# Decay matrices of a two-way SSD scan: built by VectorE from broadcast rows, or as TensorE products onto a mask in PSUM

## The chip, the cores and the metric

The kernel runs on one core of one Trainium2 chip. The metric is the device time of one execution in microseconds (us). Before the change it is 1887.61 us, the median of three runs (1885.88 to 1889.07). Five engines work side by side, each in its own fixed order: TensorE (PE; its weight loads are PEld), VectorE (DVE), ScalarE (ACT), GpSimd (POOL), and SyncE (SP), which in this kernel issues every DMA.

## The reference

One layer of a hybrid block over 1024 latent tokens of width 1024, with a context of 256 tokens: a modulated RMSNorm, one wide input projection, three branches (a bidirectional Mamba-2 SSD, a Fourier mix, a gated MLP over token chunks), an output projection, and a gated feed-forward with a short convolution. The change is within the SSD, which works on 8 chunks of 128 tokens, 16 heads of width 64 and 2 groups. Cut to what matters:

```
cum  = cumsum(dt * a)                                  # per head, in a chunk
lmat = exp(where(tri_q, cum[q] - cum[s], -inf))        # decay from token s to token q, 128 x 128 per head
cb   = C_q . B_s                                       # one 128 x 128 matrix per chunk and group
y_diag = sum_s cb[q,s] * lmat[q,s] * dt[s] * x[s]      # forward; the same on flipped tokens for backward
y_off  = exp(cum[q]) * C_q . state ;  y = y_diag + y_off
```

For each chunk, group and head both directions are wanted: the forward matrix lives on one side of the diagonal, the backward matrix on the other, and the two are added (on the diagonal both count).

## The kernel before

Matrices are split into a high and a low float32r part, and each projection is three products per 128 rows of depth (helper `mm3`, L147). A projection tile of 128 output channels is 48 products of 128x512 into one of two large PSUM tiles (`ps_big`, two banks each, pool `psm` with 2 buffers). Small PSUM tiles (`ps_small`, one bank) have the tags c, c2, y and t, one buffer each.

After the context and the first group's tiles, `ssd_group(0)` is written, then `group_in(1)` (the projection, convolution and transposes of the second group: tiles B, C and four x tiles, with the four Fourier tiles `f_tile` between them), then `ssd_group(1)`, then the z, u and v tiles. A scheduler merges this into one fixed order per engine. So the projection tiles ("fill tiles" here: `psx`, `psf`, `psz`, `psu`, `psv` by their PSUM names) stand on TensorE between the small products of the SSD groups. A fill x tile goes: 48 products into `psx`; `conv5` (L288: one ScalarE pass, then four VectorE passes that read `psx`); a tanh and a product (`silu_half`); eight transposes `pstx` (`tok_major`, L441) and their copies out.

One chunk step of `ssd_group` (L547 to L583): `pcb` is cb; `po` and `pS` are the products for y_off and for the state, in both directions; `py` is the product of the decay matrices with x. Per half group of four heads (`hg`) the decay matrix comes from two DMA broadcasts of rows of cum (`rload`), per head a ScalarE pass that adds the column's own cum (L561), a VectorE pass with the minimum of both directions (L562), a ScalarE and a VectorE pass for the factor with cb and dt (L564, L565), then one Exp for four heads (L567) and a product on GpSimd (L568). `ro` (L498) are decay rows for y_off, also broadcast by DMA.

Of the kernel before, what the change touches and what calls it, by code (L numbers as in the profile page):

```python
# [32 lines left out]
def hybrid_block_kernel(ctx: ExitStack, tc: tile.TileContext, a, dbg=None):  # L33
# [26 lines left out]
    def bc(ap, shape):  # L60
        return ap.broadcast_to(shape)
# [430 lines left out]
    def rload(c, d_, g, hg, nm, tag):  # L492
        r = s3.tile([P, 4, P], F32, tag=tag, name=f"{nm}{g}{c}{hg}")
        o = d_ * 16 + g * 8 + hg * 4
        SY.dma_start(r, Rd[c, o:o + 4, :].partition_broadcast(P))
        return r
# [37 lines left out]
    def xload(g, c, nm):  # L534
        X = s3.tile([P, 512], F32, tag="X" + nm, name=f"X{nm}{g}{c}", bufs=2 if nm == "f" else 1)
        SY.dma_start(X, Xd[g][c])
        return X

    def ssd_group(g, BT, Bt, CT):
        st0 = []  # L540
        for d_ in range(2):
# [4 lines left out]
        scr[1, g] = s3.tile([P, L], F32, tag="scr", name=f"scr1{g}", bufs=1)
        for c in range(NCH):  # L547
            X = xload(g, c, "f")
            pcb = ps_small(f"pcb{g}{c}", "c")
            PE.matmul(pcb[:, 0:P], BT[:, c * P:(c + 1) * P], CT[:, c * P:(c + 1) * P], start=True, stop=True)  # L550
            cbm = s3.tile([P, 2, P], F32, tag="cbm", name=f"cbm{g}{c}", bufs=1)
            V.tensor_tensor(cbm, bc(pcb[:, 0:P].unsqueeze(1), [P, 2, P]), msk, op=ALU.mult)  # L552
            y_off(g, c, 0, stf, CT, G)
            py = ps_small(f"py{g}{c}", "y")
            for hg in range(2):
                E = rload(c, 0, g, hg, "rf", "rf")
                rs = rload(c, 1, g, hg, "rs", "rs")
                Gm = s3.tile([P, 4, P], F32, tag="G", name=f"G{g}{c}{hg}")
                for h in range(4):
                    f = g * 8 + hg * 4 + h  # L560
                    S.activation(E[:, h, :], E[:, h, :], AF.Identity, bias=ncum[:, c, f:f + 1])  # L561
                    V.scalar_tensor_tensor(E[:, h, :], rs[:, h, :], ncum[:, c, 16 + f:17 + f], E[:, h, :],  # L562
                                           op0=ALU.add, op1=ALU.min)
                    S.activation(Gm[:, h, :], cbm[:, 0, :], AF.Copy, scale=dtl[:, c, f:f + 1])  # L564
                    V.scalar_tensor_tensor(Gm[:, h, :], cbm[:, 1, :], dtl[:, c, 16 + f:17 + f], Gm[:, h, :],  # L565
                                           op0=ALU.mult, op1=ALU.add)
# [30 lines left out]
    xbc_post(10, psb10, CT)  # L597
    n2w, nfw, ssdd, ssdn, fcw, fcb = late_consts()
    Rd = dram.tile([NCH, 32, P], F32, name="Rd")
    psr = ps_small("psr")  # L600
    for i in range(2):
        PE.transpose(out=psr[:, i * P:(i + 1) * P], in_=cums[:, 4 * i:4 * i + 4, :].rearrange("p c h -> p (c h)"),
                     identity=ident)
    Rs_ = ddp.tile([P, 2, P], F32, tag="ul", name="Rs_")
    S.activation(Rs_, psr[:, 0:2 * P].rearrange("p (i q) -> p i q", i=2), AF.Copy)
    SY.dma_start(Rd.rearrange("(i c) h q -> (c h) i q", i=2), Rs_)
    yacc[0] = mpool.tile([P, 4, L], F32, tag="m", name="yacc0")
    for i, ts in enumerate(((9,), (4, 5), (6,), (7,))):
        x_tile(0, i, True)
# [1135 lines left out]
```

## Time and profile before

| | |
|---|---|
| median of three runs | 1887.61 us |
| the profiled execution | 1883.76 us, its span 1882.0 us, mean granted TensorE clock 0.967 |
| busy in the span | PE 1747.4 us (93%), DVE 1383.9 (74%), ACT 859.9 (46%), POOL 856.0 (45%) |
| the SSD groups with their fill tiles | 235.7 to 558 us of the span |

A view by lines gives, per group of equal instructions, the busy time, the mean ns of one, and the idle time of the engine before them with what ended it. A view by windows gives, for a stretch of time, the busy time of each engine and its count of instructions.

### The profile page before, as it was taken

What the parts mean: (1) busy time and instruction counts of PE and PEld (TensorE: products, weight loads), DVE (VectorE), ACT (ScalarE), POOL (GpSimd) and SP (SyncE); (2) the same over time, 40 slices, a digit from 0 to 9 for tenths busy, and PEclk for the clock granted to TensorE, in tenths of its full rate; (3) what the DMA queues carried; (4) which work ended last, traced back from release to release, by engine and by line L of the source; (5) the groups of instructions that cost most, each with busy time, mean ns of one, the idle gap of its engine ahead of it and who ended that gap; (6) DMA issues with size and microseconds to landing.
All of it is one profiled execution on the core that took longest, in us unless ns stands there. A gap on an engine that the chain in (4) does not pass through costs nothing. (4 is left out here: it accounts for less than half of the span.)

```text
span 1882.0 us, 23647 instructions
## 1 busy us (share of the span) xinstructions
PE 1747.4 (93%) x8148; PEld 1409.2 (75%) x8148; DVE 1383.9 (74%) x1983; ACT 859.9 (46%) x1480; POOL 856.0 (45%) x579
## 2 busy tenths in 40 slices
PE   4899998988989989999899999799999999899988
PEld 2688776766668868888688888578888888677777
DVE  7875577777573675557949536998888889967896
ACT  6644355564442344444524234445555455533433
POOL 3322355556531464554645745633333333544553
PEclk9999999999999989999998999899999999999998
DMA  9211365553454225765346464122232225553532
GB/s 336 101 59 61 118 191 159 154 159 116 148 183 160 107 85 184 235 224 184 118 146 201 129 230 140 40 90 96 95 126 104 96 96 174 199 187 106 174 111 90
DMA packets 148064, 268.75 MB, mean 143 GB/s; under 512 B 15836, under 2 KB 56668, under 8 KB 146536
## 3 DMA queue, kind: packets, MB, share of 16 engines
q1 hardware_dynamic: 147944, 267.25, 43.0%
q8 instruction: 64, 1.05, 0.2%
q14 instruction: 56, 0.46, 0.1%
HBM read 209.90 MB, written 57.29 MB: 142 GB/s over the span
## 5 line engine op out<-in xcount | busy, mean ns | idle before, releaser
L293 DVE SCALAR_TENSOR_TENSOR acc<-psx,convw,acc 128x1023 f32<-128x1023 f32 (+1 forms) x48 | 61.3, 1277 | 22.5 <-ACT acc L289 22.1
L562 DVE SCALAR_TENSOR_TENSOR rf<-rs,ncuml,rf 128x128 f32<-128x128 f32 x128 | 52.2, 454 | 32.4 <-ACT rf L561 29.2
L1272 POOL TENSOR_TENSOR pwo<-rwo,pwo 128x512 fp32r<-128x512 f32 x32 | 46.8, 1467 | 48.5 <-ACT pwo L1271 43.4
L857 POOL TENSOR_TENSOR w1up<-A11up,w1up 128x512 fp32r<-128x512 f32 x20 | 26.8, 1342 | 89.8 <-ACT w1up L856 80.6
L568 POOL TENSOR_TENSOR rf<-rf,G 128x512 f32<-128x512 f32 x32 | 46.1, 1442 | 43.1 <-DVE G L565 33.0
L857 POOL TENSOR_TENSOR w7up<-S3up,w7up 128x512 fp32r<-128x512 f32 x20 | 28.8, 1438 | 77.5 <-ACT w7up L856 45.0
L565 DVE SCALAR_TENSOR_TENSOR G<-cbm,dtl,G 128x128 f32<-128x128 f32 x128 | 57.0, 504 | 5.1 <-ACT G L564 5.1
L1561 DVE SCALAR_TENSOR_TENSOR xf<-Yd,g,xf 128x512 f32<-128x512 f32 x64 | 47.1, 743 | 13.0 <-PE Yd L867 12.7
L561 ACT ACTIVATE rf<-rf,ncuml 128x128 f32<-128x128 f32 x128 | 41.1, 389 | 29.5 <-DMA rf<-Rd 29.3
L166 ACT ACTIVATE gh<-gr 128x1024 fp32r<-128x1024 f32 (+1 forms) x36 | 37.1, 1034 | 38.0 <-DMA gr<-Gd 37.1
L157 PE MATMUL pso<-mh,pwo 128*128 128x512 f32 x128 | 50.2, 392 | 0.0
L153 PE MATMUL pso<-mh,pwo 128*128 128x512 f32 x128 | 49.8, 390 | 0.0
L155 PE MATMUL pso<-ml,pwo 128*128 128x512 f32 x128 | 49.8, 389 | 0.0
L517 DVE TENSOR_TENSOR scr<-po,ro 128x512 f32<-128x512 f32 x32 | 21.8, 683 | 35.2 <-ACT ro L504 35.0
L527 PE MATMUL pS<-scr,Bt 128*128 128x512 f32 x56 | 32.9, 671 | 15.4 <-DVE scr L517 12.0
L504 ACT ACTIVATE ro<-ro 128x512 f32<-128x512 f32 x32 | 20.1, 627 | 57.4 <-DMA ro<-Rd 57.1
L564 ACT ACTIVATE G<-cbm,dtl 128x128 f32<-128x128 f32 x128 | 39.6, 388 | 7.4 <-DVE cbm L552 7.4
L167 DVE TENSOR_TENSOR gl<-gr,gh 128x1024 fp32r<-128x1024 f32 (+1 forms) x26 | 39.7, 1527 | 4.2 <-ACT gh L166 3.6
L1477 DVE TENSOR_TENSOR gt<-gt,aa 128x512 f32<-128x512 f32 x44 | 42.5, 967 | 0.1
L1474 ACT ACTIVATE ft<-aa 128x512 f32<-128x512 f32 x44 | 27.8, 631 | 30.0 <-DVE aa L1456 29.0
L529 POOL TENSOR_TENSOR st<-st,etl 128x512 f32<-128x512 f32 x24 | 26.5, 1106 | 31.6 <-DVE st L531 31.6
L857 POOL TENSOR_TENSOR w4up<-A22up,w4up 128x512 fp32r<-128x512 f32 x20 | 30.9, 1544 | 21.4 <-ACT w4up L856 21.4
(1291 smaller groups left out, 6622.6 us busy)
## 6 DMA issues: line engine op xcount, KB each, us to landing
gr<-Gd SPq DMA_DIRECT2D x70, 256.0 KB, 3.7
Gd<-gt SPq DMA_DIRECT2D x10, 1536.0 KB, 5.7
wm<-in_wmod_dram SPq DMA_DIRECT2D x16, 512.0 KB, 9.6
ro<-Rd SPq DMA_DIRECT2D x64, 128.0 KB, 3.3
rf<-Rd SPq DMA_DIRECT2D x32, 256.0 KB, 4.3
rs<-Rd SPq DMA_DIRECT2D x32, 256.0 KB, 3.8
ctanh<-in_wmod_dram SPq DMA_DIRECT2D x32, 256.0 KB, 4.3
crow<-in_wmod_dram SPq DMA_DIRECT2D x32, 256.0 KB, 4.4
```

Of the source, the lines that this page charges most:

```text
L153: PE.matmul(o, wh[:, k, :], xh[:, sl], start=st, stop=False)
L155: PE.matmul(o, wh[:, k, :], xl[:, sl], start=False, stop=False)
L157: last_op["mm"] = PE.matmul(o, wl[:, k, :], xh[:, sl], start=False, stop=sp)
L293: V.scalar_tensor_tensor(acc[:, lo:hi], ps[:, lo + o:hi + o], cw[:, t, j:j + 1], acc[:, lo:hi], op0=ALU.mult, op1=ALU.add)
L561: S.activation(E[:, h, :], E[:, h, :], AF.Identity, bias=ncum[:, c, f:f + 1])
L562: V.scalar_tensor_tensor(E[:, h, :], rs[:, h, :], ncum[:, c, 16 + f:17 + f], E[:, h, :], op0=ALU.add, op1=ALU.min)
L565: V.scalar_tensor_tensor(Gm[:, h, :], cbm[:, 1, :], dtl[:, c, 16 + f:17 + f], Gm[:, h, :], op0=ALU.mult, op1=ALU.add)
L568: G.tensor_tensor(E, E, Gm, op=ALU.mult)
L857: (V if p in on_v else G).tensor_tensor(t[:, 1, :], ap, f32(t)[:, 0, :], op=ALU.subtract)
L1272: G.tensor_tensor(t[:, 1, :], raw, f32(t)[:, 0, :], op=ALU.subtract)
L1477: V.tensor_tensor(gt[:, 2 * q + h, :], gt[:, 2 * q + h, :], aa[:, HS[h]], op=ALU.mult)
L1561: V.scalar_tensor_tensor(xv, src, g2[:, dd:dd + 1], xv, op0=ALU.mult, op1=ALU.add)
```

## The change

The factor dt goes into the exponent: its logarithm (`lds`) less cum is a row per token s, cum a row per token q, and both are written to DRAM as a high and a low part (`Rr`). The exponents of four heads are then one product on TensorE: weights `Lt` of 128 rows, of which 18 are not zero (16 of lds - cum for 8 heads in two parts, 2 of ones), against `Rt` of 128 x 1024 (rows of indicators, and two rows of cum). ScalarE first writes the mask (0 or -1e30) into a PSUM bank (tag t, which nothing else uses in the SSD groups now), and the product is added onto it. ScalarE takes the Exp, VectorE adds the two directions and multiplies with cb. Tag t is no longer free for the transposes of the second group's tiles: they take a large PSUM tile in rotation with the projections.

```diff
     def tok_major(src, nm, dst, tags=("t", "t")):
+        pb = ps_big(f"pst{nm}") if tags is None else None
         for i in range(2):
-            p_ = ps_small(f"pst{nm}{i}", tags[i])
+            p_ = ps_small(f"pst{nm}{i}", tags[i]) if tags else pb[:, 512 * i:512 * i + 512]
...
+        if not tags:
+            S.activation(dst, pb.rearrange("p (c x) -> p c x", c=8), AF.Copy)
...
-        tok_major(ac, f"x{t}", xt_, ("t", "c2" if ctx_too else "t"))
+        tok_major(ac, f"x{t}", xt_, ("t", "c2") if ctx_too else None)
...
-        tok_major(BT, f"b{g}", Bt)
+        tok_major(BT, f"b{g}", Bt, None)
...
+    def exponents(E, c, d_, hg):
+        S.activation(E.rearrange("p (h q) -> p h q", h=4), bc(neg[:, d_].unsqueeze(1), [P, 4, P]), AF.Copy)
+        PE.matmul(E, Lt[c // 2 % 2][:, 2 * (c % 2) + d_, :], Rt[:, 512 * hg:512 * hg + 512], start=False, stop=True,
+                  skip_group_check=True)
+
+    def load_rows(c, g):
+        for d_ in range(2):
+            i = 2 * (c % 2) + d_
+            SY.dma_start(f32(Lt[c // 2 % 2])[32 * i:32 * i + 16, i, :],
+                         Rr[1][c, 2 * d_ + g].rearrange("l h q -> (l h) q"))
+            SY.dma_start(f32(Rt)[32 * i + 16:32 * i + 18], Rr[0][c, 2 * d_ + g].rearrange("l h q -> l (h q)"))
...
             X = xload(g, c, "f")
+            load_rows(c, g)
...
-            cbm = s3.tile([P, 2, P], F32, tag="cbm", name=f"cbm{g}{c}", bufs=1)
-            V.tensor_tensor(cbm, bc(pcb[:, 0:P].unsqueeze(1), [P, 2, P]), msk, op=ALU.mult)
+            cb = s3.tile([P, P], F32, tag="cb", name=f"cb{g}{c}")
+            S.activation(cb, pcb[:, 0:P], AF.Copy)
...
             for hg in range(2):
-                E = rload(c, 0, g, hg, "rf", "rf")
-                rs = rload(c, 1, g, hg, "rs", "rs")
-                Gm = s3.tile([P, 4, P], F32, tag="G", name=f"G{g}{c}{hg}")
-                for h in range(4):
...
-                S.activation(E, E, AF.Exp)
-                G.tensor_tensor(E, E, Gm, op=ALU.mult)
+                ef = s3.tile([P, 512], F32, tag="ef", name=f"ef{g}{c}{hg}", bufs=1)
+                E = ps_small(f"F{g}{c}{hg}", "t")
+                exponents(E, c, 0, hg)
+                S.activation(ef, E, AF.Exp)
+                eb = ps_small(f"E{g}{c}{hg}", "t")
+                exponents(eb, c, 1, hg)
+                S.activation(eb, eb, AF.Exp)
+                V.tensor_tensor(eb, ef, eb, op=ALU.add)
+                w_ = s3.tile([P, 4, P], F32, tag="G", name=f"G{g}{c}{hg}")
+                V.tensor_tensor(w_, eb.rearrange("p (h q) -> p h q", h=4), bc(cb.unsqueeze(1), [P, 4, P]), op=ALU.mult)
...
+    lds = ddp.tile([P, NCH, 32], F32, name="lds", tag="w" + "l")
+    V.tensor_scalar(lds, dtl, 1e-37, None, op0=ALU.max)
+    S.activation(lds, lds, AF.Ln)
+    V.tensor_tensor(lds, lds, cums, op=ALU.subtract)
...
+    for j in range(2):
+        rh = ddp.tile([P, 2, P], F32R, tag=("rl", "t2l")[j], name=f"rh{j}")
...
+                SY.dma_start(Rr[j][4 * i:4 * i + 4, :, q], f32(t)[:, i, :])
```

The new orders follow at three places. First, TensorE at the end of the x tile of `wx5` in the first SSD group. Before:

```order
L155 MATMUL psx_2845<-hl_549,wx5h 128x512 x2
L157 MATMUL psx_2845<-hh_548,wx5l 128x512 x2
L573 MATMUL py_1980<-rf_1981,Xf_1963 64x128 x4
L527 MATMUL pS_2037<-scr_1667,Bt_591 128x512
L153 MATMUL psf_2924<-hh_289,wf3h 128x512 x2
L155 MATMUL psf_2924<-hl_290,wf3h 128x512 x2
```

Now (F and E are the exponent products of the two directions):

```order
L155 MATMUL psx_2735<-hl_549,wx5h 128x512 x2
L157 MATMUL psx_2735<-hh_548,wx5l 128x512 x2
L498 MATMUL E_1974<-Rt,Lt_1694 128x512
L537 MATMUL pS_2083<-scr_1705,Bt_591 128x512
L561 MATMUL pcb_2113<-CT_592,BT_590 128x128
L581 MATMUL py_1968<-G_1979,Xf_1947 64x128 x4
L498 MATMUL F_1986<-Rt,Lt_1694 128x512
L498 MATMUL E_1990<-Rt,Lt_1694 128x512
L446 MATMUL pstx_2795<-cst,acc_2784 128x128 x8
L153 MATMUL psf_2812<-hh_289,wf3h 128x512 x2
```

The transposes of the same tile now stand ahead of the first product of the next fill tile; before, the whole next tile (48 products) stood between the last product of `psx` and its transposes.

Second, TensorE near the end of the second SSD group. Before, the last two `py` stand among products of the v tile `wv1`:

```order
L155 MATMUL psv_4727<-hl_438,wv1h 128x512
L573 MATMUL py_3843<-rf_3844,Xf_3826 64x128 x4
L155 MATMUL psv_4727<-hl_438,wv1h 128x512
L157 MATMUL psv_4727<-hh_437,wv1l 128x512 x2
L153 MATMUL psv_4727<-hh_474,wv1h 128x512 x2
L155 MATMUL psv_4727<-hl_475,wv1h 128x512 x2
L573 MATMUL py_3843<-rf_3871,Xf_3826 64x128 x4
L183 MATMUL rby_4462<-dgy_4456,cst 128x512
L157 MATMUL psv_4727<-hh_474,wv1l 128x512 x2
```

Now the last product of that v tile is followed by this (the first `py` here is the second half of chunk 3 of 8):

```order
L157 MATMUL psv_4467<-hh_548,wv1l 128x512 x2
L581 MATMUL py_3285<-G_3312,Xf_3264 64x128 x4
L498 MATMUL F_3367<-Rt,Lt_1693 128x512
L524 MATMUL po_3438<-CT_2338,st_3402 128x128 x4
L498 MATMUL E_3371<-Rt,Lt_1693 128x512
L537 MATMUL pS_3499<-scr_3023,Bt_2337 128x512
L537 MATMUL pS_3480<-scr_3022,Bt_2337 128x512
L524 MATMUL po_3569<-CT_2338,st_3501 128x128 x4
L581 MATMUL py_3365<-G_3376,Xf_3344 64x128 x4
L498 MATMUL F_3383<-Rt,Lt_1693 128x512
```

Chunks 4 to 7 of the second group, eight pairs of F and E with nine `py`, five `po` and four `pS`, now stand behind the last fill product; the next fill product (`psv` of `wv2`) comes after the Fourier products that follow them.

Third, SyncE at the same place, chunks 6 and 7, now (`Rt` is the load of two rows for each direction, `tabc`, `fT` and `tab` are for the Fourier products that come next):

```order
L506 DMA Rt<-Rr_866 2x1024 x2
L546 DMA Xf_3504<-Xd_581 128x512
L513 DMA ro_3639<-Rd 64x4x128 x2
L768 DMA wsT_4362<-in_wsT_dram 128x128
L770 DMA bsb_4364<-in_bs_dram 128x128
L768 DMA wsT_4457<-in_wsT_dram 128x128
L770 DMA bsb_4459<-in_bs_dram 128x128
L506 DMA Rt<-Rr_866 2x1024 x2
L546 DMA Xf_3584<-Xd_581 128x512
L506 DMA Rt<-Rr_866 2x1024 x2
L1200 DMA Hb_5024<-Hr_252 128x512
```

Each chunk's pair of `Rt` loads stands once, behind a wait for the last exponent product of the chunk before, since all products read all rows of `Rt`.

## Rows read from the trace of the kernel before

**Rows 1.** Windows: length, then busy us (count) per engine, granted clock, DMA.

```profile
235.70:404.00 168.30, 150.28 (x789) 115.08 (x787) 122.19 (x230) 95.97 (x216) 83.85 (x62) 0.99 0.58 165
404.00:558.00 154.00, 137.84 (x667) 101.83 (x668) 107.31 (x186) 75.00 (x166) 91.26 (x66) 0.93 0.47 142
...
720.00:760.00 40.00, 40.00 (x178) 33.11 (x178) 21.65 (x45) 16.71 (x30) 20.20 (x15) 1.00 0.66 211
```

**Rows 2.** Waits of PE, 200 to 560 us: us in total, times, longest.

```profile
PE pS L527 <- DVE scr L517: 12.0, 8, 3.4
```

**Rows 3.** Lines, 235 to 556 us, VectorE, ScalarE and GpSimd in the SSD.

```profile
L565 DVE SCALAR_TENSOR_TENSOR G<-cbm,dtl,G 128x128 f32<-128x128 f32 x128 | 57.0, 504 | 5.1 <-ACT G L564 5.1
L562 DVE SCALAR_TENSOR_TENSOR rf<-rs,ncuml,rf 128x128 f32<-128x128 f32 x128 | 52.2, 454 | 32.4 <-ACT rf L561 29.2 <-DMA rs<-Rd 2.9
L568 POOL TENSOR_TENSOR rf<-rf,G 128x512 f32<-128x512 f32 x32 | 46.1, 1442 | 43.1 <-DVE G L565 33.0 <-PE psx L157 6.2 <-DVE rf L562 3.1
L561 ACT ACTIVATE rf<-rf,ncuml 128x128 f32<-128x128 f32 x128 | 41.1, 389 | 29.5 <-DMA rf<-Rd 29.3
...
L517 DVE TENSOR_TENSOR scr<-po,ro 128x512 f32<-128x512 f32 x32 | 21.8, 683 | 35.2 <-ACT ro L504 35.0 <-issue 0.2
...
L567 ACT ACTIVATE rf<-rf 128x512 f32<-128x512 f32 x32 | 19.9, 623 | 19.7 <-DVE rf L562 19.5
```

**Rows 4.** The same view, TensorE's products in the SSD.

```profile
L527 PE MATMUL pS<-scr,Bt 128*128 128x512 f32 x56 | 32.9, 671 | 15.4 <-DVE scr L517 12.0 <-POOL scr L524 3.4
L514 PE MATMUL po<-CT,st 128*128 128x128 f32 x224 | 31.9, 290 | 6.4 <-DVE st L531 4.5 <-DVE cbm L552 1.7
...
L573 PE MATMUL py<-rf,Xf 128*64 128x128 f32 x256 | 20.4, 284 | 5.5 <-POOL rf L568 5.5
...
L153 PE MATMUL psx<-hh,wx5h 128*128 128x512 f32 x16 | 5.1, 398 | 0.0
```

**Rows 5.** The same view, the chain behind a fill x tile.

```profile
L293 DVE SCALAR_TENSOR_TENSOR acc<-psx,convw,acc 128x1023 f32<-128x1023 f32 x10 | 12.8, 1279 | 4.7 <-ACT acc L289 4.6
...
L297 ACT ACTIVATE tmp<-acc 128x1024 f32<-128x1024 f32 x5 | 5.2, 1048 | 2.4 <-DMA Xd<-xt 2.4
...
L298 DVE SCALAR_TENSOR_TENSOR acc<-tmp,acc 128x1024 f32<-128x1024 f32 x4 | 4.9, 1217 | 1.7 <-ACT tmp L297 1.7
L289 ACT ACTIVATE acc<-psx,convb,convw 128x1024 f32<-128x1024 f32 x4 | 4.8, 1194 | 0.0
```

**Rows 6.** PE in order of time at the end of x tile wx4.

```profile
264.09 0.62 PE L153 MATMUL psf<-hh,wf2h 128*128 128x512 f32 x2
...
284.72 0.60 PE L445 MATMUL pstx<-cst,acc 128*128 128x128 f32 x4
```

**Rows 7.** All engines in order of time: ScalarE to TensorE, TensorE to ScalarE.

```profile
308.42 1.02 ACT L454 ACTIVATE fs<-psf 128x1024 f32<-128x1024 f32 x1 [1.10 <-DMA Xd<-xt]
309.85 1.84 PE L153 MATMUL psf<-hh,wf3h 128*128 128x512 f32 x2
...
553.68 1.12 PE L183 MATMUL rby<-dgy,cst 128*128 128x512 f32 x2
554.85 0.60 ACT L185 ACTIVATE rby<-rby 128x512 f32<-128x512 f32 x1 [0.39 <-PE rby L183]
```

**Rows 8.** The line that writes rows of cum, 128 KB to DRAM.

```profile
DMA to landing us min/median/max: 1.8/1.8/1.8
```

**Rows 9.** SyncE and PE in order of time.

```profile
553.83 0.33 SPq L691 DMA_DIRECT2D tabc<-in_tabc_dram  x1
...
558.01 3.02 PE L707 MATMUL psF<-tabc,fT 128*128 128x128 f32 x24
```

**Rows 10.** Windows as in rows 1, with a stall of 3.44 us.

```profile
400.00:408.00 8.00, 4.56 (x11) 2.40 (x10) 7.32 (x10) 5.07 (x12) 5.24 (x4) 0.76 0.64 178
```

**Rows 11.** Lines of ScalarE: the load of a function table.

```profile
L115 ACT ACT_TABLE_LOAD x1 | 1.3, 1283 | 0.7 <-PEq L1735 0.7
```

**Rows 12.** PE in order of time: the wait for the weights wc5.

```profile
140.05 0.39 PE L157 MATMUL psc<-hch,wc5l 128*128 128x256 f32 x1 [2.19 <-POOL wc5l L139]
```

More of the change, by code (lines that the diff above doesn't have):

```diff
@@ L446, in tok_major @@
                              identity=ident)
-            S.activation(dst[:, 4 * i:4 * i + 4, :], p_.rearrange("p (c x) -> p c x", c=4), AF.Copy)
+            if tags:
+                S.activation(dst[:, 4 * i:4 * i + 4, :], p_.rearrange("p (c x) -> p c x", c=4), AF.Copy)
+        if not tags:
+            S.activation(dst, pb.rearrange("p (c x) -> p c x", c=8), AF.Copy)
     def f_tile(g):
@@ L490, in group_in @@
         return BT, Bt, CT
[L492 to L496, printed above, removed]
+    def exponents(E, c, d_, hg):
[8 more added lines that the diff above has]
+            SY.dma_start(f32(Rt)[32 * i + 16:32 * i + 18], Rr[0][c, 2 * d_ + g].rearrange("l h q -> l (h q)"))
     def decay_rows(c, d_, g):
@@ L555, in ssd_group @@
             for hg in range(2):
-                E = rload(c, 0, g, hg, "rf", "rf")
-                rs = rload(c, 1, g, hg, "rs", "rs")
-                Gm = s3.tile([P, 4, P], F32, tag="G", name=f"G{g}{c}{hg}")
-                for h in range(4):
[L560 to L566, printed above, removed]
-                S.activation(E, E, AF.Exp)
-                G.tensor_tensor(E, E, Gm, op=ALU.mult)
+                ef = s3.tile([P, 512], F32, tag="ef", name=f"ef{g}{c}{hg}", bufs=1)
[8 more added lines that the diff above has]
+                V.tensor_tensor(w_, eb.rearrange("p (h q) -> p h q", h=4), bc(cb.unsqueeze(1), [P, 4, P]), op=ALU.mult)
                 for h in range(4):
@@ L572, in ssd_group @@
                     i = 2 * hg + h // 2
-                    PE.matmul(py[64 * j:64 * j + 64, i * P:(i + 1) * P], X[:, hd:hd + 64], E[:, h, :],
+                    PE.matmul(py[64 * j:64 * j + 64, i * P:(i + 1) * P], X[:, hd:hd + 64], w_[:, h, :],
                               start=True, stop=True)
@@ L599, in hybrid_block_kernel @@
     Rd = dram.tile([NCH, 32, P], F32, name="Rd")
+    Rr = [dram.tile([NCH, 4, 2, 8, P], F32, name=f"Rr{i}") for i in range(2)]
     psr = ps_small("psr")
-    for i in range(2):
-        PE.transpose(out=psr[:, i * P:(i + 1) * P], in_=cums[:, 4 * i:4 * i + 4, :].rearrange("p c h -> p (c h)"),
+    lds = ddp.tile([P, NCH, 32], F32, name="lds", tag="w" + "l")
+    V.tensor_scalar(lds, dtl, 1e-37, None, op0=ALU.max)
+    S.activation(lds, lds, AF.Ln)
+    V.tensor_tensor(lds, lds, cums, op=ALU.subtract)
+    for i in range(4):
+        PE.transpose(out=psr[:, i * P:(i + 1) * P],
+                     in_=(cums, lds)[i // 2][:, 4 * (i % 2):4 * (i % 2) + 4, :].rearrange("p c h -> p (c h)"),
                      identity=ident)
+    pr4 = psr.rearrange("p (i q) -> p i q", i=4)
     Rs_ = ddp.tile([P, 2, P], F32, tag="ul", name="Rs_")
-    S.activation(Rs_, psr[:, 0:2 * P].rearrange("p (i q) -> p i q", i=2), AF.Copy)
+    S.activation(Rs_, pr4[:, 0:2], AF.Copy)
     SY.dma_start(Rd.rearrange("(i c) h q -> (c h) i q", i=2), Rs_)
+    for j in range(2):
+        rh = ddp.tile([P, 2, P], F32R, tag=("rl", "t2l")[j], name=f"rh{j}")
+        rl = ddp.tile([P, 2, P], F32R, tag=("ql", "lal")[j], name=f"rl{j}")
+        S.activation(rh, pr4[:, 2 * j:2 * j + 2], AF.Copy)
+        V.tensor_tensor(rl, pr4[:, 2 * j:2 * j + 2], f32(rh), op=ALU.subtract)
+        for q, t in enumerate((rh, rl)):
+            for i in range(2):
+                SY.dma_start(Rr[j][4 * i:4 * i + 4, :, q], f32(t)[:, i, :])
     yacc[0] = mpool.tile([P, 4, L], F32, tag="m", name="yacc0")
@@ L618, in hybrid_block_kernel @@
     s3 = pool("s3", bufs=2, side="right")
+    neg = s3.tile([P, 2, P], F32, name="neg", bufs=1)
+    V.tensor_scalar(neg, msk, -1.0, 1e30, op0=ALU.add, op1=ALU.mult)
+    Rt = s3.tile([P, L], F32R, name="Rt", bufs=1)
+    ind = s3.tile([P, L], F32, tag="scr", name="ind", bufs=1)
+    SY.dma_start(ind, a["ind"])
+    S.activation(Rt, ind, AF.Copy)
+    Lt = [s3.tile([P, 4, P], F32R, name=f"Lt{i}", bufs=1) for i in range(2)]
+    ltc = s3.tile([P, 4, P], F32, tag="ef", name="ltc", bufs=1)
+    SY.dma_start(ltc, a["ltc"])
+    for i in range(2):
+        S.activation(Lt[i], ltc, AF.Copy)
+    PE.matmul(ps_small("E0", "t"), Lt[0][:, 0, :], Rt[:, 0:512], start=True, stop=True)
     ssd_group(0, *gi)
@@ L1694, in prepare @@
     r["tabc"], r["tabl"] = tabc, tabl
+    ind = np.zeros((4, 32, 8, P), np.float32)
+    for h in range(8):
+        ind[:, [h, h + 8], h] = 1.0
+    r["ind"] = ind.reshape(P, L)
+    ltc = np.zeros((4, 32, 4, P), np.float32)
+    for q in range(4):
+        ltc[q, 16:18, q] = 1.0
+    r["ltc"] = ltc.reshape(P, 4, P)
     wm = i["w_mod"][0]
```

## Prediction

> **What bounds the kernel now.** I read the windows first. In the two SSD groups with their fill tiles (235.7 to 558 us) TensorE is busy 150.28 of 168.30 and 137.84 of 154.00 us; VectorE, the next, 122 and 107 [rows 1]. So TensorE bounds the stage with 18.0 + 16.2 = 34.2 us of stalls in it, and that is all that a lighter VectorE, ScalarE or GpSimd can give. In a stretch without stalls TensorE issues 178 products of 512 columns in 40 us, one per 0.225 us [rows 1]. The waits say where the stalls come from: the longest is `pS` waiting for VectorE's `scr`, 12.0 us in 8 times [rows 2], that is, products of the SSD that stand in TensorE's order before their inputs are there. Everything behind 558 us is again nearly all TensorE and waits for the SSD's y, so a delay in this stage reaches the end in full.
>
> **What goes.** On VectorE 128 passes of 454 ns and 128 of 504 ns (109 us), on ScalarE 128 of 389 ns and as many of L564, which are alike, on GpSimd 32 of 1442 ns (46 us) [rows 3], and 64 broadcast DMAs. None of that bounds the stage; it frees TensorE only where a stall hangs on it, so it is worth between 0 and 34.2 us, and I keep this as one term: stalls that are left among fill products.
>
> **What comes on TensorE.** 64 exponent products (8 chunks, 2 groups, 2 halves, 2 directions) of 128 rows by 512 columns in float32r, at 0.225 us: +14.4 us of TensorE work. The few rows that are not zero do not make them shorter. On VectorE come 64 passes like L517 (683 ns, 44 us) [rows 3], so it is 65 us lighter in all; ScalarE gets 64 mask writes and 32 more Exps for 256 short passes, about even. Whatever these cost beside fill products is hidden; where no fill product is at hand, it is not.
>
> **The step of tag t.** One bank serves both directions of both halves, so it is a serial loop: mask write, product, Exp, mask write, product, Exp, add, multiply, and only then the next mask write. From rows: four ScalarE passes of 0.62 us (L567) and two VectorE passes of 0.68 us (L517) [rows 3], two products of 0.40 us from start to end (L153) [rows 4], and the handoffs: ScalarE to TensorE 309.85 - (308.42 + 1.02) = 0.41 us, twice; TensorE to ScalarE 554.85 - (553.68 + 1.12) = 0.05 us, twice; ScalarE to VectorE and back about as much [rows 7]. Sum 2.48 + 1.36 + 0.80 + 1.0 = 5.6 us per half chunk. Its bounds are 4.6 us (no handoff) and 7 us (both VectorE passes queued behind two other SSD passes of 0.68 us). No row of before shows ScalarE writing PSUM or a mask seeded there; the pass of the same size out of SBUF is the nearest. The Trainium skill ("ScalarE: Activation LUTs", section "Step-by-step: what each stage is for") calls PSUM the faster destination for ScalarE; it gives no figure, and each 0.1 us off the three PSUM writes of a step would take 8 x 0.3 = 2.4 us off the tail below, a result of about 1938 us.
>
> **The tail.** In the new order the fill products end when chunks 4 to 7 of the second group still have their eight F and E pairs to go; before, the last `py` stood among fill products. The next v tile can't fill in: its PSUM tile and its buffer wait for the SSD's end, then as before. So eight steps run with only the SSD's own products beside them: 8 x 5.6 = 45 us, 2 us for the last add, multiply and `py`, and 0.5 us a chunk where the `Rt` loads are late. These wait for the chunk's last product, and the bank's own way to the next product (Exp, two VectorE passes, mask write, handoffs) takes about 3.2 us; two issues of 0.33 us [rows 9] and a landing, 1.8 us for the nearest DMA [rows 8], take 2.5 us, or 4.3 us if it lands in twice that, so 0 to 1.1 us a chunk is open. 49 us in all. Of TensorE's work in it, nine `py` (8 x 20.4 / 256 = 0.64 us), five `po` (8 x 31.9 / 224 = 1.14), four `pS` (2 x 32.9 / 56 = 1.18) [rows 4] and 16 exponent products (3.6) make 20 us. Left idle: +29 us (18 with 4.6 us steps, 42 with 7 us).
>
> **The gaps at fill tiles.** Before, `psf` of the next tile starts the moment an x tile's products end (264.09 us), and the transposes of that x tile come 20 us later (284.72) [rows 6]. Now the transposes, in the large PSUM tile, stand ahead of the next fill products, and TensorE, which works in order, waits for the whole chain behind the x tile: L289 1.19, four L293 at 1.28, L297 1.05, L298 1.22 us [rows 5], two fours of transposes 1.2 us [rows 6], handoffs 0.4: 10.2 us, with a VectorE pass of the SSD in between 10.5 us and more. Inside stand 4 to 8 us of SSD products (at `wx5`: three exponent products, one `pS`, one `pcb`, one `py` and the transposes, 4.2 us); 5 us of each gap is idle. The four x tiles of the second group have it: +20 us (12 to 32). Its B tile has it too, ahead of the first SSD group, with eight passes of the context's state (0.68 us, like L517) in the chain on VectorE: 10.5 + 5.4 - 7.7 us of products (six of the length of `pS`, four transposes): +8 us (4 to 10).
>
> **The small ends.** (a) Behind the SSD the Fourier products wait for DMAs that start when its memory is free; before, that took from 553.83 to 558.01 us [rows 9], all under products of the last v tile. Uncovered but for the norm's products: +3 us (0 to 6). (b) SyncE has eight more DMAs (the rows' parts) ahead of the load of weights `wc5`, for which TensorE waits 2.19 us already [rows 12]: 8 x 0.33 = 2.6 us later, partly behind other products: +2 us (0 to 5). (c) ScalarE gets a Ln between Exps: two more table loads of 1.28 us [rows 11], and ScalarE is busy for only 46% of the span: nothing (up to 2.6 us if TensorE waits for it). The Trainium skill ("ScalarE: Activation LUTs", section "What ACT_TABLE_LOAD costs") adds a drain of about 1.38 us to each load, 2.66 us a switch, 5.3 us for both. The row shows the load's 1283 ns and no drain beside it; if the drain came on the path too, the sum would be 5 us higher. (d) Stalls left among fill products: F and E add four places per chunk at which TensorE can wait for ScalarE or VectorE, but most pairs have 20 or more fill products between them, more than the 1.5 to 2.5 us that they need: +8 us (0 to 30), against the -34.2 us of before.
>
> **The clock.** The granted clock is 0.99 and 0.93 in the two groups [rows 1]: 1.7 + 10.8 = 12.5 us of full-speed time lost. It falls from the 2.4 to the 1.2 GHz level around stalls: the mean is 0.76 in the 8 us with a stall of 3.44 us [rows 10]. Now five gaps of about 1.5 us of such loss, the tail with TensorE under half busy (its exponent products 0.2 us longer, 16 times) and 3 us behind it, and a few for the rest: about 18.5 us, so +6 us (0 to 14).
>
> **Sum.** 14.4 + 29 + 20 + 8 + 3 + 2 + 8 - 34.2 + 6 = +56 us on the profiled execution's 1883.8 us: **1940 us**. That execution lies 3.9 us under the median of the three runs, within their spread nearly, so the same number stands against 1887.6: 2.8% slower.
>
> **Rivals.**
> 1. Relief wins (the other side). VectorE 65 us and GpSimd 46 us lighter, no stall on `scr` or `rf` any more. For it: the longest wait on TensorE hangs on VectorE [rows 2]. It takes off at most 34.2 us and pays 14.4; it decides if gaps, tail and clock together cost under 20 us, which needs the x tiles' chain to be covered and the steps to run in half the time of their rows. With 15 us for both: 1883.8 - 34.2 + 14.4 + 15 = 1879 us. Against it: the orders fix both idles. Chance 0.06.
> 2. The loop is late among fill products too. ScalarE stands in order: mask writes and Exps are queued behind passes on weights that wait for DMAs, which stand on SyncE behind the `Rt` loads, which wait for TensorE. If each of the 24 steps outside the tail costs TensorE 1.3 us, +31 us: 1971 us. For it: the stage already loses 34.2 us to such queues. Against: the fill products between pairs. Chance 0.24.
> 3. Even: stalls among fill go to zero, gaps cost 3 us each (15 with the B tile), the tail's steps 4.6 us (18), small ends and clock nothing: 14.4 + 15 + 18 - 34.2 = +13, 1897 us; only with half the gaps does it end within 0.2% of before. Chance 0.08, of which 0.04 within.
>
> The forecast itself has 0.62, with its own range 1912 to 1965 us. For 8 in 10 I take 1902 to 1980 us: it leaves out rival 1, half of rival 3 and the upper third of rival 2. 0.2% (3.8 us) is about what a measurement of this kernel can tell from no change. Faster 0.06, same 0.04, slower 0.90.
>
> **What would show it.** In the changed trace: TensorE idle 4 us or more ahead of each `pstx` of the second group, released by VectorE L298; a stretch of 45 to 55 us ahead of `psF` with TensorE under half busy and eight F and E pairs 5 to 6 us apart; exponent products of about 0.23 us at the full clock; VectorE's busy time 60 us less, GpSimd's 46 us less; granted clock under 0.9 in the tail. The forecast is wrong if the pairs in the tail come 3 us apart or less, if fill products run at `pstx` time after all, or if TensorE waits for F and E among fill products for more than 25 us.

## The result, and the profile after

The changed kernel takes 1943.09 us (median of 4 runs, 1941.56 to 1946.75) against 1888.03 us (four runs, three of which gave the 1887.61 us above): a ratio of 1.0296, 95% interval 1.0278 to 1.0314. The forecast was 1940 us, 2.8% slower. The profiled execution's span is 1941.9 us, 59.9 us more than before.

The page's row of busy times: VectorE has 70 us less than before and GpSimd 53 us less, TensorE 33 us more.

```profile
PE 1780.2 (92%) x8215; PEld 1434.0 (74%) x8215; DVE 1314.0 (68%) x1780; ACT 847.5 (44%) x1339; POOL 803.2 (41%) x547
```

The windows of the changed kernel from the first product on the context's state to the first Fourier product (length, then busy us of each engine, granted clock, DMA), cut where TensorE begins or ends to stand idle:

```profile
203.88:229.13 25.25, 19.37 (x68) 11.97 (x67) 15.70 (x20) 5.76 (x7) 3.93 (x3) 0.93 0.42 134
229.13:281.00 51.87, 51.87 (x261) 40.54 (x259) 24.58 (x30) 22.25 (x36) 25.31 (x21) 1.00 0.49 140
281.00:293.07 12.07, 7.07 (x39) 6.06 (x38) 8.75 (x9) 7.37 (x11) 4.40 (x5) 0.72 0.29 90
293.07:321.36 28.29, 28.29 (x140) 22.52 (x139) 5.95 (x9) 9.02 (x14) 7.68 (x6) 1.00 0.31 96
321.36:333.76 12.40, 5.77 (x24) 3.25 (x23) 9.26 (x10) 8.10 (x11) 4.64 (x4) 0.74 0.21 64
333.76:364.69 30.93, 30.93 (x143) 24.16 (x142) 9.32 (x17) 10.02 (x17) 8.36 (x7) 0.94 0.31 95
364.69:378.75 14.06, 10.67 (x58) 7.89 (x56) 10.44 (x12) 8.48 (x12) 5.48 (x4) 0.76 0.38 114
378.75:393.00 14.25, 13.55 (x71) 10.89 (x68) 4.04 (x6) 5.97 (x10) 3.78 (x3) 1.00 0.26 75
393.00:407.84 14.84, 7.16 (x35) 5.48 (x36) 10.36 (x12) 8.18 (x13) 1.29 (x2) 0.59 0.19 56
407.84:547.20 139.36, 139.36 (x675) 110.32 (x673) 53.62 (x63) 56.77 (x80) 58.73 (x43) 0.99 0.31 98
547.20:600.60 53.40, 30.44 (x142) 18.09 (x140) 24.19 (x34) 22.10 (x38) 11.64 (x9) 0.71 0.17 50
600.60:613.00 12.40, 7.24 (x23) 4.99 (x22) 4.04 (x7) 0.60 (x1) 2.03 (x1) 0.50 0.77 252
```

Three things are to be seen. In the windows of fill products TensorE never waits: 51.87 of 51.87, 28.29 of 28.29, 139.36 of 139.36 us; of the stalls of before [rows 1, 2] none is left there. At the B tile (the first row) and the four x tiles (the rows with a clock of 0.59 to 0.76, and 0.7 us in the one at 378.75) it is idle for 29.3 us. Behind the last fill product come 53.4 us with 23.0 idle at a clock of 0.71, and 12.4 more with 5.2 idle at 0.50.

The waits of TensorE from 203.88 to 547.20 us (total, times, longest), the answer to [rows 2]:

```profile
PE py L581 <- DVE G L576: 11.5, 4, 4.7
PE pS L406 <- DVE ctxm L403: 5.2, 2, 3.2
PE E L498 <- ACT E L497: 3.9, 4, 1.9
PE F L498 <- ACT F L497: 2.9, 1, 2.9
PE pS L537 <- POOL scr L534: 2.2, 1, 2.2
...
PE pstx L446 <- DVE acc L298: 1.4, 1, 1.4
```

The transposes themselves (`pstx`) wait for 1.4 us only. What is late in the x tiles' gaps is for the most part the step of tag t (`G`, `E`, `F`), which the order has put there bare, with VectorE's passes of the convolution between its own; at the third x tile it is a state product that waits for GpSimd's `scr`, 2.2 us.

One step of the tail, all engines in order of time, the loop whose length the prediction had added up:

```profile
587.35 0.60 ACT L497 ACTIVATE F<-neg 128x512 f32<-128x512 f32 x1 [1.49 <-DVE G L576]
587.37 1.12 PE L581 MATMUL py<-G,Xf 128*64 128x128 f32 x8 [2.13 <-DVE G L576]
588.42 0.80 PE L498 MATMUL F<-Rt,Lt 128*128 128x512 f32 x1
589.25 0.60 ACT L570 ACTIVATE ef<-F 128x512 f32<-128x512 f32 x1 [1.30 <-PE F L498]
589.88 0.60 ACT L497 ACTIVATE E<-neg 128x512 f32<-128x512 f32 x1
590.54 0.80 PE L498 MATMUL E<-Rt,Lt 128*128 128x512 f32 x1 [1.32 <-ACT E L497]
591.37 0.58 ACT L573 ACTIVATE E<-E 128x512 f32<-128x512 f32 x1 [0.89 <-PE E L498]
591.98 0.70 DVE L574 TENSOR_TENSOR E<-ef,E 128x512 f32<-128x512 f32 x1 [2.75 <-ACT E L573]
592.71 0.69 DVE L576 TENSOR_TENSOR G<-E,cb 128x512 f32<-128x512 f32 x1
593.44 0.60 ACT L497 ACTIVATE F<-neg 128x512 f32<-128x512 f32 x1 [1.49 <-DVE G L576]
...
594.56 0.80 PE L498 MATMUL F<-Rt,Lt 128*128 128x512 f32 x1
```

From mask to mask it is 6.09 us. Nothing in the loop overlaps: `py` runs beside the mask, and F waits for `py` to end. Both exponent products take 0.80 us here; among fill products one is issued every 0.22 us:

```profile
296.39 0.39 PE L498 MATMUL E<-Rt,Lt 128*128 128x512 f32 x1
296.61 1.02 PE L537 MATMUL pS<-scr,Bt 128*128 128x512 f32 x2
```

The end of the stage, in order of time:

```profile
600.65 3.57 PE L190 MATMUL psq<-cst,qz 128*128 128x1 f32 x16
606.57 2.03 POOL L175 TENSOR_TENSOR rry<-rvy,expo 128x8 f32<-128x8 f32 x1 [25.05 <-DVE rvy L173]
609.38 3.78 PE L183 MATMUL rby<-dgy,cst 128*128 128x512 f32 x4 [5.16 <-DVE dgy L180]
612.96 1.24 PE L742 MATMUL psF<-tabc,fT 128*128 128x128 f32 x5
```

The y norm of the first group (`psq`, a GpSimd pass of 2.03 us, `dgy`, `rby`), which stood among fill products before, now runs bare. Its `psq` began 100 us ahead of the Fourier products in the kernel before:

```profile
458.37 0.72 PE L190 MATMUL psq<-cst,qz 128*128 128x1 f32 x6
```

`psq` is itself a tile of tag t (`ps_small("psq0", "t")` in the kernel). So the exponents aren't alone with this bank: one other tile needs it in the time of the second SSD group, and since they hold it to their last step, the norm now starts behind that step. The Fourier products wait behind the norm, not for the DMAs of [rows 9].

### The profile page after: what moved, and what is told of

Same layout as the page of the kernel before. It is cut to its first block, busy times and chain, and to the rows that moved or that the text cites. A ratio compares the mean times of both kernels' runs of the same rounds, so it can differ in the third digit from the quotient of the medians.

```text
span 1941.9 us, 23356 instructions
## 1 busy us (share of the span) xinstructions
PE 1780.2 (92%) x8215; PEld 1434.0 (74%) x8215; DVE 1314.0 (68%) x1780; ACT 847.5 (44%) x1339; POOL 803.2 (41%) x547
## 3 DMA queue, kind: packets, MB, share of 16 engines
q1 hardware_dynamic: 141320, 252.30, 39.3%
## 5 line engine op out<-in xcount | busy, mean ns | idle before, releaser
L892 POOL TENSOR_TENSOR w1up<-A11up,w1up 128x512 fp32r<-128x512 f32 x20 | 26.7, 1337 | 88.4 <-ACT w1up L891 79.2
L574 DVE TENSOR_TENSOR E<-ef,E 128x512 f32<-128x512 f32 x32 | 22.1, 692 | 55.9 <-ACT E L573 55.9
L166 ACT ACTIVATE gh<-gr 128x1024 fp32r<-128x1024 f32 (+1 forms) x36 | 37.1, 1033 | 39.9 <-DMA gr<-Gd 34.1
L534 POOL TENSOR_TENSOR scr<-Xf,wdl 128x512 f32<-128x512 f32 x14 | 15.5, 1109 | 88.8 <-DMA Xf<-Xd 86.2
L514 ACT ACTIVATE ro<-ro 128x512 f32<-128x512 f32 x32 | 20.2, 631 | 68.1 <-DMA ro<-Rd 65.9
L581 PE MATMUL py<-G,Xf 128*64 128x128 f32 x256 | 25.0, 324 | 22.9 <-DVE G L576 20.7
L570 ACT ACTIVATE ef<-F 128x512 f32<-128x512 f32 x32 | 18.9, 592 | 50.6 <-PE F L498 50.6
L581 PEld LDWEIGHTS py<-G,Xf 128*64 128x64 f32 x256 | 15.9, 157 | 33.5 <-DVE G L576 22.4
L900 PE MATMUL Yup<-bhh,w7up 128*128 128x512 f32 x80 | 32.2, 403 | 7.1 <-DVE Uup L1091 7.1
```

The costliest lines, as they stand in the source:

```text
L166: S.activation(hi, src, AF.Copy)
L892: (V if p in on_v else G).tensor_tensor(t[:, 1, :], ap, f32(t)[:, 0, :], op=ALU.subtract)
L900: PE.matmul(o, w[:, 0, k, :], xh, start=first and k == 0, stop=False, skip_group_check=not first)
```

## The experiments

Theory A: the loss is idle time of TensorE where the order leaves a step of tag t bare (tail and x tiles), and the clock that falls around it; the 64 products cost only their own time. Theory B: the loop is late wherever it stands. The stage's length in each profile, from the first product on the context's state to the first Fourier product, against TensorE's busy time in it, by one window of each kernel:

| kernel | median us | ratio to before, 95% | stage us | busy | idle |
|---|---|---|---|---|---|
| before | 1888.03 | | 352.3 | 318.1 | 34.2 |
| changed | 1943.09 | 1.0278 to 1.0314 | 409.1 | 351.7 | 57.4 |
| e1 tiles held back | 1956.84 | 1.0329 to 1.0398 | 421.7 | 356.9 | 64.8 |
| e2 Exp to SBUF | 1906.94 | 1.0065 to 1.0166 | 382.6 | 342.5 | 40.1 |
| e3 transposes alone | 1939.37 | 1.0254 to 1.0315 | 408.3 | 334.6 | 73.7 |
| e4 no products | 1893.65 | 1.0024 to 1.0058 | 363.6 | 325.3 | 38.3 |
| e5 spread | 1913.52 | 1.0108 to 1.0168 | 382.6 | 339.1 | 43.5 |
| e6 small bank | 1931.95 | 1.0220 to 1.0271 | 401.5 | 349.5 | 52.0 |
| e7 e5 and e6 | 1906.90 | 1.0090 to 1.0131 | 373.3 | 337.2 | 36.1 |
| e8 e7 and e2 | 1888.36 | 1.0001 to 1.0030 | 360.3 | 333.6 | 26.7 |
| e9 late transposes | 1927.67 | 1.0195 to 1.0243 | 391.4 | 343.8 | 47.6 |
| e10 e9, all fill spread | 1899.42 | 1.0054 to 1.0093 | 370.9 | 333.8 | 37.1 |
| e11 e10 and e2 | 1882.16 | 0.9961 to 0.9993 | 347.5 | 327.0 | 20.5 |
| e12 e10, short products | 1893.31 | 1.0023 to 1.0065 | 359.9 | 323.1 | 36.8 |

Each ratio is to runs of the kernel before on the same chip; with the experiments these had medians of 1885.8 to 1886.2 us.

**e1, fill tiles held back whole.** Each z, u and v tile starts behind a given `py` of the second group.

```diff
         ps = ps_big(f"psu{g}")
-        mm3(halves(ps), wt, hx, KT)
+        with tc.issue_after(pys[1][h]):      # h = 1, 2, 4, 6, 7, 9, 10, 12, 13
+            mm3(halves(ps), wt, hx, KT)
```

> The products of the z, u and v tiles are held back in TensorE's order, so that each starts only behind a given product py of the second group; nothing else is changed, and one pair of F and E instead of eight is left behind the last fill product. Theory A (the loss is the tail, where the serial loop of bank t runs with no fill product beside it): the 23 us of idle time in the tail and some 8 us of its slow clock go, 1905 to 1917 us. Theory B (the loop is late wherever it stands, so the idle time only moves among the fill products): 1935 to 1945 us, with TensorE's waits for F, E and G among fill products larger by some 25 us.

It became slower, 1956.84 us, beyond both ranges, which taken by itself speaks for B. But the order shows why it doesn't decide: a tile is tied to a `py` only at its start, so between two tiles the steps up to the next `py` stand bare. One long tail was cut into many short ones: 24.6 us of idle time lie spread over the stretch from 408 to 600 us, with waits of E for its mask of up to 2.3 us and of `py` for `G` of up to 2.8 us. The experiment missed its aim; e5 does the same in small pieces.

**e5, the fill products spread.** The 48 products of each tile are tied in eight groups of six, each behind one F or E product, so that every step of the second group has fill beside it.

```diff
-        mm3(halves(ps), wt, hx, KT)
+        for k in range(KT):                  # j counts the groups from z0 on; from j = 8 to 79
+            with tc.issue_after(pairs[32 + (j - 8) * 4 // 9]):
+                mm3(halves(ps), (wt[0][:, k:k + 1], wt[1][:, k:k + 1]), lambda _, k=k: hx(k), 1, k == 0, k == KT - 1)
```

> The changed kernel, with the products of the z, u and v tiles tied in groups of six or less behind the F and E products of the second group, so that TensorE's order has between two of them 6 to 24 fill products and no pair behind the last fill product; nothing else is changed. Theory A (idle time comes only where a step of bank t has no fill product beside it): the tail's 23 us of idle time, some 8 us of its slow clock and a few us of the end go, 1900 to 1914 us; the gaps at the x tiles stay. Theory B (as the run with fill tiles held back whole would have it: the loop is late wherever it stands): 1935 us or more.

1913.52 us, 29.6 us less, by the order alone; as A has it. Idle time falls by 13.9 us, and busy time, for the same products, by 12.6 us: slow and lonely products are worth nearly as much as the idle time. Of the tail's 23 us some ten came back between 400 and 565 us, where the changed kernel had 2 us idle up to 547:

```profile
400.00:564.70 164.70, 152.68 (x773) 118.02 (x774) 77.93 (x100) 77.80 (x120) 66.54 (x49) 0.96 0.29 90
```

**e2, the Exp of the second direction to SBUF.**

```diff
-                S.activation(eb, eb, AF.Exp)
-                V.tensor_tensor(eb, ef, eb, op=ALU.add)
+                S.activation(wf, eb, AF.Exp)             # wf: the tile w_, in SBUF
+                V.tensor_tensor(wf, ef, wf, op=ALU.add)
```

> The Exp of the second direction goes to the SBUF tile of the product instead of back into the bank, so bank t is free after it and both VectorE passes (1.4 us and a handoff) leave the loop: a step of about 4.2 us instead of 5.7 us, and two pairs left in the tail by the order. Theory A (length of the loop times the number of steps without fill): 1900 to 1915 us, tail about 12 us. Theory B (the 64 products and their waits cost the same anywhere): 1933 to 1943 us.

1906.94 us: bank t is free two VectorE passes earlier, and the order, which follows from the kernel's text, has two steps in the tail instead of eight. The run doesn't tell these two apart; e8 and e11 do.

**e4, no products.** The call of `PE.matmul` in `exponents` is left out.

> The changed kernel without its 64 exponent products; the output leaves out the decay (Exp is taken of the mask alone). Mask writes, Exps, VectorE passes, loads and the transposes in the large tile stay; the order leaves no step behind the fill. Theory A (products 14 us, and by their place in a long loop the tail of 45 us and more): 1880 to 1897 us. Theory D (the products cost their own 14 us and little else): 1925 to 1932 us.

1893.65 us. All that the products bring, 49 us, is far over their own time; theory D is out. What is left, 0.4% over before, is the transposes' price against the relief: 36.0 of the stage's 38.3 us of idle time lie ahead of 412 us, where the last x tile ends, and the longest wait from 204 to 568 us is the transposes' own (in the kernel before, 1.2 us):

```profile
PE pstx L446 <- DVE acc L298: 18.4, 3, 9.0
```

**e12, short products**, 128 columns instead of 512, in the order of e10.

```diff
-        m = PE.matmul(E, Lt[...], Rt[:, 512 * hg:512 * hg + 512], start=False, stop=True, ...)
+        m = PE.matmul(E[:, 0:P], Lt[...], Rt[:, 512 * hg:512 * hg + P], start=False, stop=True, ...)
```

> As e10, with the 64 exponent products 128 columns wide instead of 512; the other exponents are left out (the output is not the reference's). The loop and the order stay. The products' own price: 0.225 us each at 512 columns and about a quarter of it at 128, so 64 x 0.17 = 11 us less than e10 by theory A; by theory B (the loop's length is what costs) 64 x 0.3 us = 20 us less.

Busy time in the stage falls from 333.8 to 323.1 us, idle time stays (37.1, 36.8). So 384 columns cost 10.7 / 64 = 0.167 us, and 512 of them, in proportion, 0.223 us: an estimate of 14.3 us for the 64, as forecast, though only 18 of 128 rows are not zero. (The medians differ by 6.1 us, less than either theory, with spreads of 9 and 13 us; over the whole execution TensorE's busy time falls by 8.6 us.)

**e3, the large transposes alone**, in the kernel before.

```diff
-        tok_major(ac, f"x{t}", xt_, ("t", "c2" if ctx_too else "t"))
+        tok_major(ac, f"x{t}", xt_, ("t", "c2") if ctx_too else None)
-        tok_major(BT, f"b{g}", Bt)
+        tok_major(BT, f"b{g}", Bt, None)         # tags None: the large tile
```

> The kernel before, with the old decay matrices, and of the change only the transposes of the second group's five tiles in the large PSUM tile. Theory A (a gap of 5 to 7 us at each of five tiles because the next tile's products stand behind the transposes): 1908 to 1922 us. Theory C (the gaps are waits for the F and E loop, which happens to stand there): within 5 us of before, 1885 to 1893 us.

1939.37 us: 54 us over before, more than either theory. This one edit costs the old kernel what the whole change costs. Waits from 230 to 560 us:

```profile
PE pstx L446 <- DVE acc L298: 17.3, 2, 9.0
PE py L577 <- POOL rf L572: 15.4, 6, 7.4
PE pS L531 <- DVE scr L521: 12.5, 7, 3.2
```

The stalls of before are still there (`scr`), the transposes wait 17.3 us, and `py` now waits bare for GpSimd's product, up to 7.4 us. From 203 us to the transposes of the last x tile at 433 us TensorE is idle for 57.7 us; the same tiles in the changed kernel hold 29.3 us. What differs there is the work of the SSD (over the stage VectorE is busy for 256.5 us in e3 and 180.2 us in the changed kernel), so the gaps and the relief are not terms of their own.

**e6, transposes in a small bank** (tag c2, that of the backward state).

```diff
-        tok_major(ac, f"x{t}", xt_, ("t", "c2") if ctx_too else None)
+        tok_major(ac, f"x{t}", xt_, ("t", "c2") if ctx_too else ("c2", "c2"))
-        tok_major(BT, f"b{g}", Bt, None)
+        tok_major(BT, f"b{g}", Bt, ("c2", "c2"))
```

> The changed kernel, with the transposes of the second group's five tiles in a small bank (that of the backward state products) instead of the large PSUM tile, so the next fill tile's products again stand ahead of them; 6.5 steps instead of 8 are left in the tail. Theory A (gaps of 29 us idle at five tiles, 5.7 us a step of tail): 29 us and about 8 us less, 1900 to 1912 us. Theory E (the small bank is needed by the state products, and the wait comes back there): 1930 to 1945 us.

1931.95 us, in E's range. The B tile's gap is gone, but 25 us of idle time stay from 230 to 400 us, and the tail with the norm is 59 us:

```profile
204.80:230.00 25.20, 25.20 (x101) 18.41 (x100) 13.55 (x16) 5.08 (x6) 5.56 (x4) 1.00 0.36 115
230.00:400.00 170.00, 145.08 (x688) 108.24 (x687) 78.85 (x102) 77.64 (x122) 54.52 (x43) 0.89 0.34 101
...
547.00:606.30 59.30, 32.21 (x131) 20.29 (x130) 20.14 (x31) 17.86 (x31) 7.91 (x5) 0.61 0.27 83
```

E's reason isn't what the waits show. From 204.8 to 400 us the transposes wait for copies out of their bank 1.7 us in all, and no state product waits for one; the longest waits are still for `G` and, new, for ScalarE's copy of a Fourier tile:

```profile
PE py L581 <- DVE G L576: 7.6, 5, 3.9
PE psx L153 <- ACT fs L458: 4.6, 2, 3.0
```

**e9, late transposes.** They stay in the large tile, but are written behind the products of the next fill tile.

```diff
-        for i in range(4):
-            x_tile(g, i)
-            filler()
+        for i in range(4):
+            ac = x_front(g, i, pn if i == 3 else xbc_mm(4 * g + i)[0])
+            pn = f_mm(2 + i) if i < 2 else xbc_mm(4 * g + 3)[0] if i == 2 else None
+            x_back(g, i, ac)                     # transposes of x tile i
+            if i < 2: f_out(2 + i, pn)
```

> The changed kernel, with the transposes of the second group's tiles written (still in the large PSUM tile) only behind the products of the next fill tile, and the Fourier tile's copy in another SBUF buffer; nothing holds the fill products back, and the order has nine steps of bank t in the tail instead of eight. Theory A (gap and tail are separate terms): the gaps' 23 us of idle time (B tile and x tiles) mostly go, one step of 5.7 us more in the tail: 1920 to 1930 us. Theory F (the SSD's steps that have no fill beside them are only moved from the x tiles to the tail and elsewhere): 1938 us or more.

1927.67 us, 15 us less, in A's range. The gaps shrink from 29.3 to some 5 us, but more than half of that is lost again (the stage's idle time falls by 9.8 us only): bare steps stand between 400 and 530 us and the tail grows by a step.

```profile
205.70:400.00 194.30, 189.49 (x921) 148.53 (x920) 95.13 (x115) 81.06 (x115) 70.77 (x49) 0.97 0.38 118
400.00:530.00 130.00, 115.92 (x565) 87.89 (x563) 55.53 (x69) 58.19 (x88) 57.31 (x41) 0.95 0.31 95
530.00:597.10 67.10, 38.42 (x160) 23.86 (x161) 28.68 (x43) 22.97 (x42) 10.83 (x9) 0.61 0.27 80
```

So A has the time, and F the reason why it isn't more: fill products that are used up at the x tiles are missing later.

**e7, e8: e5 and e6 together, and with e2.**

> Both edits together: fill products tied between F and E, transposes in the small bank. Theory A (gaps, tail and products add up): 1870 to 1882 us, faster than before. Theory B or E: 1900 us or more.

> As the run before it, and the Exp of the second direction goes to SBUF, so the loop of bank t is about 1.5 us shorter. Theory A (with fill products beside every step the length of the loop no longer matters): the same as without it within 6 us, 1868 to 1882 us. Theory B (a late loop costs among the fill products too): 15 to 30 us faster than without it.

1906.90 and 1888.36 us: A's 1870 to 1882 us was wrong, and B right on the shorter loop, which gives 18.5 us (in the two profiles 20.0 us, 13.0 of it in the stage). In e8 TensorE also waits for the loads of `Rt`, 3.6 us in three waits, which it does neither in e7 nor in the changed kernel. **e10 and e11** cover the steps of both groups (late transposes, and all fill tiles of the first group but the first tied likewise, `pairs[j // 2]`), without and with e2.

> Late transposes, and the products of all fill tiles of both groups tied behind F and E products, 12 to 18 fill products between two of them, so nearly no step of bank t stands bare. Theory A (products 14 us against stalls of 34 us, gaps and tail removed): 1866 to 1882 us, faster than before. Theory B (the loop is late among fill products too): 1890 us or more.

> As the run before it, and the Exp of the second direction goes to SBUF (a step shorter by about 1.5 us). Theory A: the same within 6 us. Theory B: 10 us or more faster than without it.

1899.42 and 1882.16 us, both as B has it: again 17 us for the shorter loop. The waits of TensorE from 230 us to the tail's place show it, of e10 first and then of e11:

```profile
PE F L517 <- ACT F L516: 13.1, 10, 4.2
PE E L517 <- ACT E L516: 4.2, 1, 4.2
```

```profile
PE E L517 <- ACT E L516: 4.1, 3, 2.5
PE F L517 <- ACT F L516: 3.5, 3, 1.3
```

From E's end to the next F the loop has Exp, two VectorE passes, a mask and the handoffs, 594.56 - (590.54 + 0.80) = 3.2 us in the step shown above; 12 fill products (2.7 us at 0.225) with a `py` just cover that, and not where a pass of a fill tile is ahead on VectorE or ScalarE. Without the two VectorE passes in the bank's loop the waits for F fall from 13.1 to 3.5 us. e11 is the one version faster than before, by 0.2% (interval 0.1 to 0.4%).

## Why the prediction was right

The time is right, and the cause is where the prediction put it; but three terms were missed by 6 to 9 us each, in both directions, and 4 us came behind the stage.

| step of the prediction | forecast us | measured |
|---|---|---|
| 64 products' own time | +14.4 | +14.3 (e12, an estimate) |
| stalls of before | -34.2 | -34.2 |
| stalls left among fill products | +8 | 0 (windows of 100% busy) |
| gaps at four x tiles, B tile | +20, +8 | +23.4, +5.9 idle |
| tail, idle | +29 | +23.0 |
| behind the SSD | +3 | 12.4 us long, 5.2 idle |
| early `wc5` | +2 | no wait for it; the stretch before 203.9 us is 1.8 us shorter, with 3.1 us less work in it |
| clock | +6 | +15 in the stage (an estimate) |
| behind the first Fourier product | 0 | +4.2, of which 2.7 busy and 1.5 idle |

The measured rows go into the span so: the idle time of the stage is 57.4 - 34.2 = 23.2 us more, its busy time 351.7 - 318.1 = 33.6 us more. Of these 14.3 are the products'; 3.1 are 13 products of the first Fourier tile (`psf` of `wf0`), which stood ahead of the stage before and stand in it now; 16.2 are products that take longer. Behind it 146.8 us from 612.96 us to the first product with `w3g` (759.72) stand against 142.6 before (558.01 to 700.56), the rest is 0.7 us longer and the stretch before 1.8 us shorter: 23.2 + 33.6 + 4.2 + 0.7 - 1.8 = 59.9 us.

- **The step that was mis-sized most is the clock.** I worked it out from the loss in a window with one stall and put +6 us, with 3.2 us for the tail, where I let only the 16 exponent products become longer. TensorE's busy time in each window above, times what its granted clock lacks to 1, makes 26.0 us; [rows 1] give 11.1 us for before. That is +15 us, an estimate, with 8.8 us in the tail and 3.6 behind it: every product there is longer. The tail is 53.4 us (forecast 49), and TensorE is busy for 30.4 us of it, not 20, so it isn't under half busy as I had said. That the sum came out is owed to the opposite errors, which is luck: 8 us of stalls that never came, 6 us less idle time in the tail.
- **The loop** came to 5.7 to 6.1 us between the last five F (forecast 5.6), again by errors that cancel. In the step above the six passes take 3.77 us (forecast 3.84), but the two products 1.60 us, not 0.80, the handoffs 0.25 us in all, not 1.0, and `py`, which the sum left out, holds F back for 0.47 us. Over all eight the F are (594.56 - 548.01) / 7 = 6.65 us apart, not 5 to 6, with the widest, 10.3 us, behind the first, where the state products wait as well:

```profile
548.01 0.50 PE L498 MATMUL F<-Rt,Lt 128*128 128x512 f32 x1
```

  `Rt` was not late in this kernel: TensorE has no wait for it.
- **The gaps** have the size, but not the mark in the trace that I named. I looked for 4 us ahead of each `pstx`, released by VectorE's L298; it is 1.4 us once. The SSD products that I counted as work inside the gap are themselves the waiting ones. Where the order puts none of them there the mark is as I said, two waits of 8.3 and 9.0 us in e3 and two of 9.0 us in e4. e9 shows what this means: the gap is no term of its own, since most of it moves when it is removed.
- **Behind the SSD** I named the DMAs of the Fourier products; it was the y norm, whose first product needs bank t. The text ahead of the prediction says that nothing else uses this bank in the SSD groups; `psq` does, in the time of the second.
- **Rival 2** (the loop is late among fill products) was wrong for this order, where two products of tag t in the fill stand 6 to 10 us apart, and right for the denser ones that have no tail (e8, e10). **Rival 1** needed both idles covered and the steps halved; e11, which comes nearest to that, gains 0.2%, about 4 us. That the relief and the gaps hang together (e3: +54 us without the relief, e4: +8 us with it) stood in none of the terms.
- On the Trainium skill: "ScalarE: Activation LUTs", section "Step-by-step: what each stage is for", calls PSUM the faster destination of ScalarE. The trace agrees, by little: the Exp of the second direction, out of PSUM and back into it, takes 582 ns and that of the first, out of PSUM to SBUF, 592; L514's from SBUF to SBUF takes 631, the masks from SBUF into PSUM 595 to 601. The same page's section "What ACT_TABLE_LOAD costs" adds a drain of 1.38 us to a load; no row shows one: the Ln begins 1.30 us behind the start of its load, which follows the pass before it at once.

```profile
116.23 1.21 ACT L289 ACTIVATE acc<-psx,convb,convw 128x1024 f32<-128x1024 f32 x1 [1.93 <-PE psx L157]
117.45 1.28 ACT L612 ACT_TABLE_LOAD   x1
118.75 0.42 ACT L612 ACTIVATE lds<-lds 128x256 f32<-128x256 f32 x1
```

What stays open: how much of e11's remaining 20.5 us of idle time could still be covered, whether the transposes could share bank t with the exponents, and what of the 12.4 us behind the tail would go if `psq` had another bank. No run shows any of this.

## What to carry to other kernels

A change that takes work from other engines is judged on the bounding engine: count what it must now wait for in its own order, and give each link of a serial chain through one buffer its row. A chain longer than the work that the order puts beside it shows up as idle time wherever the cover ends, so shorten the chain (free the bank at the first read: e2, 36 us by two lines and the order that follows from them) before spreading the cover. Look, too, for every other user of a buffer that is given to a new loop (`psq` here). And charge idle time of TensorE with what it does to the products beside it: between e11, whose row is this, and the changed kernel idle time grows by 39.3 us over the whole execution, from 122.4 to 161.7 us, and the same 8215 products by 26.9 us.

```profile
PE 1753.3 (93%) x8215; PEld 1416.4 (76%) x8215; DVE 1327.2 (71%) x1780; ACT 848.2 (45%) x1339; POOL 818.2 (44%) x547
```

## What the runs showed of the hardware that was not expected

- Idle time of TensorE came with two thirds as much again in longer products (26.9 / 39.3 above), and in the stage of e5 with nearly as much (12.6 for 13.9 us). The granted clock stood at 0.50, the 1.2 GHz level, in the 12.4 us behind the tail and already in the tail's last 13.3 us, where no wait is longer than 2.2 us. It was 0.99 to 1.00 in stretches that were 100% busy, but 0.94 in the one that begins at 333.76 us, right behind a gap.
- A product onto a mask that ScalarE had written into the bank costs what any product of 512 columns does, 0.22 us, and a ScalarE pass that reads or writes PSUM takes no longer than one from SBUF to SBUF (0.58 to 0.60 against 0.63 us).
